# An encoder kernel whose body is built in an inner context that orders its instructions by another timing model

## The chip, the core and the metric

The kernel runs on one core of one Trainium2 chip. The metric is the device time of one execution in microseconds, as the median of several runs.

## The reference

A trunk of one layer is applied to two sequences, of 256 and 512 tokens, with 1024 channels. Cut to what matters:

```python
h = rmsnorm(x, norm_g)
q_a, k_a, v_a, z_a, qkv_b, z_b, a_b, b_b, gate = split(h @ w_in)
y_a = diff_branch(q_a, k_a, v_a, z_a, ...)      # 8 heads: rope, two softmaxes, w = p0 - lam * p1, w @ v
y_b = gdn_branch(qkv_b, z_b, a_b, b_b, ...)     # 8 heads: conv of width 4, gated delta rule, both directions
gates = sigmoid(gate)
merged = gates[0] * (y_a @ w_branch[0]) + gates[1] * (y_b @ w_branch[1])
y = rmsnorm(x + merged @ w_out, final_g)
```

The gated delta rule works in chunks: each chunk needs the inverse of a triangular matrix, and a state is carried from one chunk to the next, forwards and backwards.

## The kernel before

All 768 tokens are held together as the normed, transposed input `hT`, in two parts (high and low) whose products are added, so a projection costs three matmuls per block. A *unit* is one projection of 128 output channels: `load_split` (L152) loads a weight tile `raw` by a DMA on SP, ACT casts it to `whi` (L149), DVE subtracts to `wlo` (L150), and 24 pairs of matmuls (L197; `pa` of 256 columns, `pb` of 512) run into two accumulators; then an epilogue on ACT and DVE reads them. `raw`, `whi` and `wlo` have two buffers each, the accumulators four.

The projections are a background stream. `step_d` (L209) issues them under a priority counter of their own that starts at 1,000,000, so each ranks behind all other work; `fill` and `fill_to` place them in the text between the steps of the foreground, and `fill(1.3, True)` gives some of them the foreground's priority. The foreground is, in order: norm and transposes of the input; four pairs of heads of the gated delta rule (`gdn_pair`), each with a convolution (`conv`, L397: a scaled copy on ACT at L406, six taps on DVE at L410, a tanh at L413 and a product at L414), transposes of `kq` (L454), decays (`gb` fetched by DMA at L518, two POOL steps at L519 and L521, an exponential `ee` on ACT at L531), an inverse (`inverse`, L549) and a scan over chunks (`scan_round`, L684: `ps_s`, `ps_x`, `ps_o` on PE, `xd`, `xn`, `o` on ACT, `r`, `S`, `o` on DVE); then eight heads of attention; then the tail, where `load_y` (L968) loads the eight tiles of a branch's result (`yr`, two buffers) and splits them into `yh` and `yl`, the branch's projections run, and `out_proj` (L997) ends the kernel.

The text is not the order on the chip. A framework collects all instructions with their dependences and priorities and, when its context closes, walks through them with a model of the machine: whenever an engine is free in the model, the instruction of the lowest priority number whose inputs and buffers are ready in the model comes next on that engine, DMA issues included. What it yields is one fixed list of instructions for each engine, with semaphores; on the chip each engine takes its list in that order. The kernel before uses the framework's default model for this, which is the simpler one of two.

Of the kernel before, what the change touches and what calls it, by code (L numbers as in the profile page):

```python
# [41 lines left out]


@with_exitstack
def tile_trunk(
    ctx: ExitStack,
    tc: tile.TileContext,
    x_prompt, x_sample, norm_g, w_in, conv_w, lam_qk, diff_norm_g, a_log, dt_bias,
# [1033 lines left out]
    hes.close()  # L1082


# [1 line left out]
_INS = ["x_prompt", "x_sample", "norm_g", "w_in", "conv_w", "lam_qk", "diff_norm_g", "a_log", "dt_bias",  # L1086
        "gdn_norm_g", "w_branch", "w_out", "final_g"]
# [32 lines left out]
```

## Time and profile before

| | |
|---|---|
| median of 3 runs | 1219.04 us (1217.39 to 1221.33) |
| the profiled execution | 1223.08 us, span 1221.2 us, mean granted TensorE clock 0.992 |
| PE busy | 1178.3 us (96%), 7952 matmuls |
| PE weight loads busy | 1034.0 us (85%) |
| DVE busy | 746.4 us (61%) |
| ACT busy | 554.7 us (45%) |
| POOL busy | 122.7 us (10%) |
| DMA | 133.60 MB in 173063 packets, mean 109 GB/s |

The span is from the first to the last instruction that the profiler recorded; the execution's own time has 1.9 us around it. Matmuls are pipelined, so a busy PE is not PE at its peak. In the rows, L12 is line 12 of the kernel file, and out<-in names the tiles that an instruction writes and reads.

### The profile page before, as it was taken

How to read it: one execution, taken by the hardware profiler on the slowest of the kernel's cores; microseconds unless marked ns; L12 is line 12 of the kernel's file. 1: busy time of each engine (PE TensorE's matmuls, PEld its weight loads, DVE VectorE, ACT ScalarE, POOL GpSimd, SP SyncE). 2: the span in 40 equal slices, each digit the busy share in tenths (PEclk: the TensorE clock that was granted, in tenths of full speed). 3: DMA queues.
4: the chain of work that ended last, by engine and by line, in shares of the span. 5: the costliest groups of instructions: out<-in, count | busy, mean ns of one | idle time of the engine just before them, and what ended most of it. 6: DMA issues, size and time to landing. Idle time of an engine off the chain costs nothing. (4 is left out here: it accounts for less than half of the span.)

```text
span 1221.2 us, 20819 instructions
## 1 busy us (share of the span) xinstructions
PE 1178.3 (96%) x7952; PEld 1034.0 (85%) x7952; DVE 746.4 (61%) x1542; ACT 554.7 (45%) x1403; POOL 122.7 (10%) x210
## 2 busy tenths in 40 slices
PE   6979998999999998999999999999999999999997
PEld 5868888888888888888899889898898888878886
DVE  5568846675566846668254657767476645457332
ACT  6454445434662346722362546656465454332011
POOL 2222013200311022110000000000000000000000
PEclk9989999999999999999999999999999999999999
DMA  5213341345223451243425554353544548444231
GB/s 179 76 50 77 85 100 32 100 127 112 63 53 98 115 115 44 55 128 102 111 85 156 146 127 135 103 138 83 143 121 112 146 160 238 151 138 121 69 113 70
DMA packets 173063, 133.60 MB, mean 109 GB/s; under 512 B 53338, under 2 KB 147876, under 8 KB 172964
## 3 DMA queue, kind: packets, MB, share of 16 engines
q1 hardware_dynamic: 172832, 132.22, 38.7%
q8 instruction: 63, 1.03, 0.4%
q14 instruction: 36, 0.29, 0.1%
q10 hardware_dynamic: 132, 0.05, 0.0%
HBM read 89.72 MB, written 23.64 MB: 93 GB/s over the span
## 5 line engine op out<-in xcount | busy, mean ns | idle before, releaser
L197 PE MATMUL pb<-hT,whi 128*128 128x512 f32 x1152 | 432.7, 400 | 0.4 <-ACT hT L142 0.3
L197 PE MATMUL pa<-hT,whi 128*128 128x256 f32 x1152 | 322.6, 287 | 1.9 <-DVE gsp L240 1.9
L197 PEld LDWEIGHTS pb<-hT,whi 128*128 128x128 f32 x1152 | 216.6, 189 | 47.3 <-ACT hT L142 0.8
L197 PE MATMUL pb<-hT,wlo 128*128 128x512 f32 x576 | 230.3, 400 | 0.0
L197 PEld LDWEIGHTS pa<-hT,whi 128*128 128x128 f32 x1152 | 216.6, 190 | 5.3 <-DVE gsp L240 2.2
L149 ACT CAST whi<-raw 128x1024 fp32r<-128x1024 f32 x88 | 92.9, 1056 | 209.5 <-PE pb L197 204.0
L197 PE MATMUL pa<-hT,wlo 128*128 128x256 f32 x576 | 165.0, 287 | 0.1
L150 DVE TENSOR_TENSOR wlo<-raw,whi 128x1024 fp32r<-128x1024 f32 x88 | 108.3, 1230 | 71.9 <-ACT whi L149 67.1
L197 PEld LDWEIGHTS pb<-hT,wlo 128*128 128x128 f32 x576 | 108.7, 189 | 23.0
L197 PEld LDWEIGHTS pa<-hT,wlo 128*128 128x128 f32 x576 | 109.1, 189 | 1.6 <-DVE wlo L150 0.3
L410 DVE SCALAR_TENSOR_TENSOR kq<-xp,pcol,kq 128x258 f32<-128x258 f32 x96 | 55.7, 634 | 27.8 <-ACT kq L406 27.8
L197 PE MATMUL pv<-vhi,hT 128*128 128x256 f32 x384 | 72.2, 284 | 0.2 <-ACT xp L803 0.2
L897 ACT ACTIVATE pw<-ps_sc,st 128x512 f32<-128x512 f32 (+1 forms) x96 | 58.2, 619 | 30.8 <-DVE st L895 30.6
L299 POOL TENSOR_TENSOR oss<-oss,mhalf 128x6 f32<-128x6 f32 x16 | 22.6, 1415 | 439.5 <-DVE oss L298 439.5
L197 PEld LDWEIGHTS pv<-vhi,hT 128*128 128x128 f32 x384 | 60.1, 188 | 1.2 <-ACT xp L803 0.5
L895 DVE TENSOR_REDUCE st<-ps_sc 128x1 f32<-128x512 f32 (+1 forms) x80 | 51.5, 684 | 8.9 <-PE ps_sc L893 8.6
L197 PE MATMUL pv<-vlo,hT 128*128 128x256 f32 x192 | 54.4, 284 | 0.0
L584 DVE TENSOR_TENSOR inv<-inv 96x31 f32<-96x31 f32 (+15 forms) x124 | 41.9, 338 | 17.8 <-ACT inv L562 14.5
L197 PE MATMUL pb<-yh,whi 128*128 128x512 f32 x128 | 51.4, 402 | 0.0
L197 PE MATMUL pb<-yl,whi 128*128 128x512 f32 x128 | 51.0, 399 | 0.0
L197 PE MATMUL pb<-yh,wlo 128*128 128x512 f32 x128 | 50.7, 398 | 0.0
L1011 PE MATMUL po<-hT,mh 128*128 128x512 f32 (+1 forms) x156 | 45.4, 374 | 0.3 <-DVE gth L956 0.3
(288 smaller groups left out, 2202.8 us busy)
## 6 DMA issues: line engine op xcount, KB each, us to landing
raw<-in_w_in SPq DMA_DIRECT2D x72, 512.0 KB, 4.1
xx<-xp SPq DMA_DIRECT2D x64, 192.0 KB, 3.4
raw<-in_w_branch SPq DMA_DIRECT2D x16, 512.0 KB, 4.0
gb<-gcd SPq DMA_DIRECT2D x16, 384.0 KB, 3.6
gtd<-gsp SPq DMA_DIRECT2D x16, 384.0 KB, 2.7
th<-xp SPq DMA_DIRECT2D x64, 96.0 KB, 2.9
gth<-gtd SPq DMA_DIRECT2D x16, 384.0 KB, 4.1
vraw<-in_w_in SPq DMA_DIRECT2D x4, 1024.0 KB, 6.6
```

The costliest lines, as they stand in the source:

```text
L149: nc.scalar.copy(whi, raw)
L150: nc.vector.tensor_tensor(out=wlo, in0=raw, in1=whi.bitcast(F32), op=ALU.subtract)
L197: nc.tensor.matmul(out, l_, r_, start=st, stop=sp)
L299: nc.gpsimd.tensor_tensor(out=oss[:, 0, :], in0=oss[:, 1, :], in1=mhalf[:, :NCH], op=ALU.pow)
L410: nc.vector.scalar_tensor_tensor(out=dst[:, a:b], in0=xp[:, w + a:w + b], scalar=cw(w), in1=dst[:, a:b], op0=ALU.mult, op1=ALU.add)
L584: nc.vector.tensor_tensor(out=tmp[:, :n, :w], in0=L[:, j + 1:, j:j + 1].to_broadcast(shp), in1=X[:, j:j + 1, :w].to_broadcast(shp), op=ALU ...
L895: nc.vector.tensor_reduce(out=st[:, c, :G], in_=ps.rearrange("p (g s) -> p g s", g=G), axis=AX.X, op=ALU.max, negate=True)
L897: nc.scalar.activation(pw[:, c, S * g_:S * g_ + S], ps[:, S * g_:S * g_ + S], AF.Exp, bias=st[:, c, g_:g_ + 1], accum_out=sums[:, c, i:i + 1])
L1011: nc.tensor.matmul(ps[:, :c1 - c0], a[:, ts_], b[:, cs], start=f, stop=l)
```

## The change

The function that builds the body is renamed, and a new function of the old name opens a critical section in the given context and, inside it, a second context on the same core. The second context is told to order its instructions by the framework's timeline model (a model of the occupancy of engines, their queues and the DMA engines, and of TensorE's clock) and not by the default one. The body is built in the inner context, with the same text, tiles, buffers and priorities. For the outer context the critical section is one item that comprises all engines.

```diff
 @with_exitstack
-def tile_trunk(
+def trunk(
     ctx: ExitStack,
     tc: tile.TileContext,
     x_prompt, x_sample, norm_g, w_in, conv_w, lam_qk, diff_norm_g, a_log, dt_bias,
@@
     hes.close()
 
 
+def tile_trunk(tc, *args):
+    with tc.tile_critical(), tile.TileContext(tc.nc, schedule_with_timeline_sim=True) as inner:
+        trunk(inner, *args)
+
+
 # ---- launch: one core; inputs and outputs as the reference has them ----
```

## Rows read from the trace of the kernel before

**Rows 1.** The page: busy us of each engine, share of the span, instructions.

```profile
PE 1178.3 (96%) x7952; PEld 1034.0 (85%) x7952; DVE 746.4 (61%) x1542; ACT 554.7 (45%) x1403; POOL 122.7 (10%) x210
```

**Rows 2.** Windows of 40 us: window, length, busy (count) by engine, clock, DMA share, GB/s.

```profile
40.00:80.00 40.00, 32.53 (x180) 28.39 (x179) 23.46 (x49) 22.34 (x60) 13.21 (x20) 0.87 0.24 68
...
240.00:280.00 40.00, 40.00 (x233) 35.01 (x232) 26.29 (x68) 11.06 (x14) 1.78 (x4) 1.00 0.42 115
```

**Rows 3.** Timeline, start: start us, us, engine, line, what [idle before <-releaser].

```profile
0.81 0.20 POOL masks.py:197 MEMSET ident<- 128x128 f32 x1 [0.29 <-POOLq L1106]
...
7.26 0.45 PE L113 MATMUL ps_par<-ident,prow 128*128 128x128 f32 x1 [7.26 <-DMA prow<-in_diff_norm_g]
```

**Rows 4.** Timeline of the end.

```profile
1214.81 0.42 DVE L1012 TENSOR_TENSOR xres<-xres,po 128x256 f32<-128x256 f32 x1 [1.72 <-PE po L1011]
...
1216.90 1.41 DVE L1020 SCALAR_TENSOR_TENSOR sqf<-xres,ss,fg 128x512 f32<-128x512 f32 x2 [0.75 <-POOL ss L1017]
```

**Rows 5.** Waits of PE, 80 to 640: total us, times, longest; first and last of seven.

```profile
PE ps_x L715 <- ACT o L726: 2.6, 1, 2.6
...
PE ps_x L715 <- DVE v L546: 0.2, 1, 0.2
```

**Rows 6.** Waits of PE, 640 to 1000: first and last of five.

```profile
PE pa L197 <- DVE gsp L240: 1.9, 1, 1.9
...
PE pv L197 <- ACT xp L803: 0.2, 1, 0.2
```

**Rows 7.** Waits of PE, 1000 to 1222: first of three.

```profile
PE pa L197 <- ACT yh L975: 1.7, 1, 1.7
```

**Rows 8.** Timeline around the wait at 73.16.

```profile
61.49 0.32 SPq L518 DMA_DIRECT2D gb<-gcd  x1
...
62.45 0.59 ACT L402 COPY xp<-pb 128x512 f32<-128x512 f32 x1
...
65.17 1.48 POOL L519 TENSOR_TENSOR gb<-gb,NGC 128x768 f32<-128x768 f32 x1 [1.72 <-DMA gb<-gcd]
...
67.62 0.84 ACT L531 ACTIVATE ee<-gb 128x768 f32<-128x768 f32 x1 [2.89 <-POOL gb L521]
68.37 0.92 ACT L406 ACTIVATE kq<-xp,pcol 128x770 f32<-128x770 f32 x1
...
69.41 3.27 DVE L410 SCALAR_TENSOR_TENSOR kq<-xp,pcol,kq 128x258 f32<-128x258 f32 x6 [4.15 <-ACT kq L406]
...
73.16 0.66 PE L454 MATMUL ps_t<-ident,kq 128*128 128x128 f32 x2 [7.47 <-DVE kq L414]
```

**Rows 9.** Line L531: what ended ACT's idle time before it (us, times).

```profile
  POOL gb L521: 13.3, 6
```

**Rows 10.** Timeline of ACT in the first scan.

```profile
188.59 0.84 ACT L531 ACTIVATE ee<-gb 128x768 f32<-128x768 f32 x1 [2.21 <-POOL gb L521]
```

**Rows 11.** Windows around the wait at 73.16.

```profile
73.00:79.00 6.00, 5.84 (x23) 5.30 (x24) 3.43 (x9) 4.97 (x18) 0.00 (x0) 0.50 0.00 0
79.00:82.00 3.00, 3.00 (x18) 2.63 (x18) 2.88 (x6) 2.94 (x16) 0.17 (x3) 0.97 0.02 7
```

**Rows 12.** Line L154, the load of a weight tile: time to landing.

```profile
DMA to landing us min/median/max: 3.7/4.1/9.4
```

**Rows 13.** The page: costliest groups, busy us, mean ns | idle before.

```profile
L149 ACT CAST whi<-raw 128x1024 fp32r<-128x1024 f32 x88 | 92.9, 1056 | 209.5 <-PE pb L197 204.0
...
L150 DVE TENSOR_TENSOR wlo<-raw,whi 128x1024 fp32r<-128x1024 f32 x88 | 108.3, 1230 | 71.9 <-ACT whi L149 67.1
```

**Rows 14.** Tile `yr`: time to landing.

```profile
DMA to landing us min/median/max: 3.9/4.9/5.9
```

**Rows 15.** Groups of PE, 992 to 1016: count, busy us, mean ns | idle.

```profile
L197 PE MATMUL pb<-hT,whi 128*128 128x512 f32 x31 | 11.2, 394 | 0.0
...
L197 PE MATMUL pb<-hT,wlo 128*128 128x512 f32 x16 | 6.4, 399 | 0.0
```

**Rows 16.** Waits of SP's queue: total us, times, longest.

```profile
SPq L154 <- DVE gsp L240: 24.1, 1, 24.1
```

## The prediction

> **What bounds the kernel now.** Busy time by engine comes first [rows 1]: of a span of 1221.2 us PE is busy 1178.3, DVE 746.4, ACT 554.7. So PE is the limit on average and its idle time is 42.9 us in all. That is the size of what any order can move, because the change neither adds nor removes a matmul. Next, the windows of 40 us [rows 2] say where PE falls short: 7.5 us in 40 to 80, nothing in 240 to 280, where only projections and the setup of the recurrence run. Part of the rest is fixed: the first matmul starts at 7.26 us, after the DMA of its operand [rows 3], and the last ends about 1214.8, 6.4 us before the end of the span [rows 4], with the last norm and store behind it. Both are chains through single instructions, and no order shortens them much.
>
> The waits of PE by stage come next: 10.0 us from 80 to 640 (seven groups, [rows 5]), where the scan of the recurrence waits for ACT and DVE; 5.5 us from 640 to 1000 (five groups, [rows 6]); 2.3 us from 1000 on (three groups, [rows 7]). With the one wait of 7.47 us at 73.16 [rows 8] this makes 25.3 us in which PE waits for another engine in the middle of the kernel.
>
> **How one of these waits arises.** The largest is the one to understand, since it shows what the order does. ACT takes `ee` (L531) at 67.62, after 2.89 us in which it stands idle for POOL's `gb` [rows 8]. The copy of the convolution (L406) stands behind it on ACT, and its input was complete when L402 ended at 63.04. DVE then starts its six taps at 69.41, having waited 4.15 us for that copy, and PE's transposes of `kq` wait for DVE. An ordering that picks, at the moment when an engine is free, the ready instruction of lowest priority number would not leave ready work standing; so when it chose `ee` its own clock must have had `gb` done. In the trace `gb` was not: its DMA was issued at 61.49 and POOL could start at 65.17, 3.7 us later, and its two steps take until ACT's start at 67.62, 2.4 us more. Over the kernel ACT stands idle before `ee` for 13.3 us, six times [rows 9], and a second of them, at 188.59, delays what stands behind it on ACT [rows 10], L726 among it, and with that the 2.6 us wait that heads [rows 5]. These are errors of the planner's durations, and durations are what the change replaces.
>
> **The change part by part.** Instructions, tiles, buffers, priorities and data stay. Three things differ.
>
> *The order.* It is chosen again on every engine and on the SP queue. I cost it by the waits it can remove.
> (a) The wait at 73.16. It costs 7.47 us, and a slower clock after it: the granted clock is 0.50 (1.2 GHz) from 73 to 79, after those 7.5 us without a matmul, and 0.97 again from 79 to 82 [rows 11]. Work of 6 us at half speed would take 3 us at 2.4 GHz, so 3.0 us more. Bounds 0 and 10.5; I take all of it, because the misjudged durations (a DMA of 3.7 us, two POOL instructions) are plain ones that a fuller model should have nearer.
> (b) The 10.0 us in the scans. Bounds 0 and 10.0; I take half, 5.0. Some are of this kind (the 2.6 us), others are links of the recurrence (`xd`, `xn`, `ma`) for which PE had no projection ready, and a better clock brings no work.
> (c) The 5.5 us of attention. Bounds 0 and 5.5; I take 2.0. The largest, 1.9 us, is a projection waiting for an accumulator that DVE has not read.
> (d) The 2.3 us of the tail, bounds 0 and 2.3; I take nothing, as they wait for loads that come one behind the other.
> (e) The new order's own waits. A model differs from the chip too, and every choice is made without looking ahead. Nothing in the trace prices this; below it is 0, above it is the 25.3 us that the present planner's errors cost. I take 4, near the lower end, since about 10.5 of those 25.3 stem from one kind of error.
>
> *The nesting.* The critical section encloses the whole body, so there is one more meeting of the engines at either end. Below, the one that the trace shows at the start: POOL is held 0.29 us [rows 3]. Above, all that follows the last DVE instruction, 1221.2 - 1218.3 = 2.9 us for the final store and the close [rows 4]. I take 1.5 us, in between; nothing hides it, as PE has no work there.
>
> *The DMA order.* Nearly all transfers are issued from SP in one order, so a transfer that waits holds those behind it. A weight tile lands in 4.1 us (median, [rows 12]) and takes 1.06 us on ACT and 1.23 us on DVE [rows 13], 6.4 us; a unit of 24 pairs of matmuls takes PE 24 x 0.343 = 8.2 us (40 us hold 233 matmuls, 116.5 pairs, [rows 2]). With two buffers of each stage the load can be up to two units ahead, so 16.4 - 6.4 = 10 us of delay is covered. I cost it at nothing, and as a rival if that cover goes.
>
> **Sum.** Against its own time, 1223.08 us (1221.2 of span and 1.9 around it): - 10.5 - 5.0 - 2.0 + 4.0 + 1.5 = - 12.0, so 1211.1 us under the profile's conditions. That execution is 4.0 us above the median of the runs, 1219.04, so I state the result as 1219.0 - 12.0 = 1207 us.
>
> **A rule set against the rows.** In 240 to 280, where PE never idles, weight loads are busy 35.01 of 40 us, 87.5% [rows 2]; over the whole kernel 1034.0 of 1221.2, 84.7% [rows 1]. If all of it ran as densely as that stretch it would take 1034.0 / 0.875 = 1181.5 us, so 39.7 us is the ceiling of any order, start and end included. The Trainium skill (Perfetto Trace Analysis, Identifying the Most-Contended Engine) says that matmul busy time is a poor measure of distance to the limit and that weight-load busy time is a good one. Read literally that leaves 15% of the span to be won (rival 4 below); the row of the dense stretch says that 12.5 of these 15.3 points are not to be had, and the trace decides.
>
> **The rivals.**
> 1. *Errors are exchanged, not removed.* The new order avoids the wait at 73.16 but makes others of the same size: (e) at 14 to 18 instead of 4. Speaking for it: 25.3 us of waits in 1221 is already little, 2.1%, and every model errs. Time: 1207 + 12 = 1219. Chance 0.13. That the order hardly differs (priorities and dependences fix it) belongs here too, with the nesting alone: 1220.5, chance 0.04. Against it: ACT's place for `ee` can only come from modelled durations.
> 2. *Slower by a cover used up.* At 992 the attention is over and the eight loads of `ybd` run in a chain: 4.9 us each with two buffers [rows 14], so some 20 us for eight. PE does not notice, because 47 pairs of projection matmuls are left (31 and 16, [rows 15]), 47 x 0.343 = 16.1 us. If the new order spends them earlier, in the waits of (b) and (c) and beyond them, PE stands up to 16.1 us and then runs at half clock for some 3 us worth, as after 73: 1207 + 19 = 1226. It passes 1222.7 when more than 13.2 of the 16.1 us are gone. For it: these matmuls have the highest numbers, that is the lowest priority, and an ordering that believes in longer waits uses them up sooner. Against it: what is spent earlier must have filled something, and only 15.5 us of waits lie between 80 and 1000. Chance 0.14.
> 3. *Slower by the SP queue.* A transfer that waits is placed ahead of a weight load for longer than the 10 us of cover. One such case stands in the trace: L154 behind `gsp`, 24.1 us [rows 16]; a wait of that length where PE has no slack costs 24.1 - 10 = 14 us. It decides from the first: 1221 with one, 1235 with two. For it: the queue is shared by nearly everything. Against it: a model with better transfer times should see just this. Chance 0.15, at 1235.
> 4. *All the time in which no weights load is to be had*, 1221.2 - 1034.0 = 187 us [rows 1], and the time nears 1034: the dense stretch above speaks against it; chance 0.01.
>
> **How the numbers follow.** The forecast, 1207 us, has 0.53; its own range is 1194 to 1215. A measurement of this kernel can tell about 0.3%, 3.7 us, from no change: faster is below 1215.4, slower above 1222.7. Faster: 0.53 + 0.01 = 0.54 and nothing of the others. Same: 0.17 from rival 1, as its times lie around 1219. Slower: 0.14 + 0.15 = 0.29. The low end is all of (a) to (d) won, 28.3 us, with 0.3 for the nesting: 1219 - 28 = 1191. The high end takes in rivals 2 and 3 with two waits and the nesting at its upper bound: 1235 + 1.4, and a few us for a third lesser wait, 1240.
>
> **What would show it.** (a) holds if PE has no wait of several us between 60 and 80 and the clock stays at 1.00 there; it fails if ACT still stands before `ee` for some 3 us. (b): fewer than 5 us of waits in the scans, with projection matmuls between `ps_x` and `ps_o`. (e): new names among PE's waits, under 5 us in sum. Nesting: more than 0.29 us before the first DMA and more than 3 us behind the last DVE instruction. Rival 2 shows as a gap of PE before `pa<-yh` with few `hT` pairs after the last `ps_yt`; rival 3 as PE waiting for `whi` or `wlo` while the load behind them was issued late. The prediction would be wrong above all if the new order makes PE wait for reasons that the present one does not have.

## The result, and the profile after

The changed kernel takes 1343.26 us (median of 4, 1342.33 to 1344.04), the kernel before, run beside it, 1220.14. The ratio is 1.1012, 95% interval 1.099 to 1.1035: 10% slower, where 1207 us was forecast and 1240 was the end of the range. The profiled execution took 1343.6 us with a span of 1341.1.

Busy time of the changed kernel, from the page; the answer to [rows 1]:

```profile
PE 1211.7 (90%) x7952; PEld 1062.5 (79%) x7952; DVE 741.0 (55%) x1542; ACT 557.7 (42%) x1403; POOL 114.3 (9%) x210
```

The instructions are the same ones (7952 matmuls), and DVE and ACT are as busy as before. PE stands idle for 1341.1 - 1211.7 = 129.4 us instead of 42.9, 86.5 more, and it is busy 33.4 us longer with the same matmuls, because more of them run at the slow clock. Four windows say where. They are, for the kernel before, start and first setup, recurrence, attention, tail (columns: window and its length, busy us and instructions of PE, PEld, DVE, ACT and POOL, granted clock of TensorE, DMA share, GB/s):

```profile
0.00:89.60 89.60, 71.60 (x382) 59.42 (x383) 53.28 (x114) 50.52 (x122) 21.83 (x51) 0.94 0.34 103
89.60:633.60 544.00, 533.34 (x4052) 467.43 (x4051) 360.06 (x892) 252.66 (x688) 82.92 (x143) 1.00 0.35 90
633.60:985.50 351.90, 348.16 (x2318) 314.30 (x2317) 221.54 (x383) 184.94 (x483) 13.33 (x9) 1.00 0.46 126
985.50:1221.20 235.70, 225.20 (x1207) 192.86 (x1206) 111.55 (x155) 66.61 (x110) 4.58 (x7) 0.99 0.41 132
```

and the same four stages of the changed kernel:

```profile
0.00:88.00 88.00, 76.00 (x435) 64.47 (x435) 54.20 (x115) 52.14 (x125) 19.57 (x50) 1.00 0.38 111
88.00:734.20 646.20, 569.58 (x4123) 499.72 (x4122) 355.97 (x899) 259.33 (x698) 77.81 (x145) 0.92 0.31 79
734.20:1114.10 379.90, 355.82 (x2312) 322.61 (x2312) 230.11 (x388) 191.23 (x491) 12.33 (x9) 0.96 0.45 122
1114.10:1341.10 227.00, 210.32 (x1089) 175.67 (x1087) 100.68 (x141) 54.97 (x90) 4.59 (x7) 0.96 0.37 117
```

The first stage is better: 53 matmuls more in 1.6 us less, at full clock. Most of the loss is in the recurrence: 102 us longer (with 71 matmuls more in it), PE idle 76.6 us instead of 10.7, clock 0.92 instead of 1.00. Attention has 24.1 us of idle instead of 3.7, the tail 16.7 instead of 10.5. The waits of PE in the changed kernel (groups as in [rows 5 to 7]: us in total, times, longest):

```profile
PE ps_y L668 <- ACT P L659: 17.0, 3, 8.2
PE ps_t L454 <- ACT kn L458: 15.1, 6, 4.3
PE ps_p L618 <- DMA XY<-sX: 13.0, 2, 12.8
PE ps_par L113 <- DMA prow<-in_diff_norm_g: 10.1, 1, 10.1
PE ps_pv L926 <- ACT wT L917: 9.0, 4, 4.1
PE ps_yt L307 <- DVE o L300: 6.0, 1, 6.0
```

Apart from `ps_par` at the start, these are names that hardly occur in the kernel before, and all of them are foreground steps: the wait of a projection would read `pa`, `pb` or `pv`. (Such waits come next in the list: 5.7 us for `gsp`, 5.3 for `vhi`, 5.0 for `zt`.) So look at the projections, PE's background work. The windows below count the matmuls of L197 alone, in the first pair's scan and in the second pair's setup; kernel before, then changed kernel (PE and PEld busy, count, clock, DMA):

```profile
179.10:210.80 31.70, 6.03 (x18) 3.06 (x18) 0.95 0.14 43
210.80:233.60 22.80, 13.94 (x65) 9.95 (x65) 1.00 0.31 99
```

```profile
202.10:264.10 62.00, 45.21 (x233) 35.43 (x232) 1.00 0.24 69
264.10:286.60 22.50, 0.60 (x2) 0.31 (x3) 0.77 0.18 59
```

The scan of the first pair now holds 233 projection matmuls instead of 18 and takes 62.0 us instead of 31.7. The setup behind it has 2 left instead of 65. Nothing is lost inside this scan: PE is busy for all of the 62.0 us, and at its end 1006 projection matmuls are done at 264.3 us where the kernel before had done 690 at 210.9. The 316 more are worth 54.2 us at 0.343 us a pair, and they took 53.4 us, so the two kernels are level there. The loss comes behind it. The setup looks like this over all engines, before and after:

```profile
210.80:233.60 22.80, 22.70 (x138) 19.01 (x136) 15.33 (x44) 15.34 (x75) 5.32 (x5) 1.00 0.31 99
```

```profile
264.10:286.60 22.50, 15.24 (x76) 11.85 (x76) 13.99 (x42) 14.67 (x73) 6.01 (x4) 0.77 0.18 59
```

The two take as long, but in the first PE was full and got 65 projection matmuls done on the side; in the second it stands 7.3 us, and the clock falls. The same happens at the next two pairs (6.1 us of idle each, clock 0.76 and 0.80). An estimate by the same 0.343 us for each pair done ahead puts the changed kernel 23 us behind the kernel before at the end of the second scan, 45 at the end of the third and 80 at the end of the fourth.

Projections are not used up for good in these setups, since hundreds of them run later; those next in line cannot start. Two finished ones hold the four accumulators until their tile `zt` is free, and `zt` is freed by the store of the pair before, which stands behind the late output transposes:

```profile
281.56 1.55 SPq L310 DMA_DIRECT2D ybd<-zt  x2
...
285.64 0.41 DVE L240 SCALAR_TENSOR_TENSOR zt<-th,pa 128x256 f32<-128x256 f32 x1
...
286.62 0.59 PE L197 MATMUL pa<-hT,whi 128*128 128x256 f32 x2
```

PE starts no projection from 265 until this one at 286.62, and the setup is all but over by then.

How the projections get into the scan shows in the timeline of the changed kernel:

```profile
208.62 0.62 ACT L734 ACTIVATE xd<-ps_x,sc__889 128x128 f32<-128x128 f32 x2 [0.76 <-PE ps_x L715]
209.13 0.37 ACT L737 COPY xn<-ps_x 128x256 f32<-128x256 f32 x1
209.23 0.48 PE L197 MATMUL pb<-hT,whi 128*128 128x512 f32 x1
...
212.01 0.28 PE L197 MATMUL pa<-hT,wlo 128*128 128x256 f32 x1
212.13 0.61 PE L744 MATMUL ps_o<-xd,kn 128*128 128x128 f32 x4
```

`xd` and `xn` are complete at 209.50. The matmuls of `ps_o` that read them start at 212.13, behind 2.6 us of projections. The order was fixed before the run, so in the model's own clock the two copies must have been done later than they are on the chip. (That is an inference; no run here changed what the model takes for ACT or PE.)

### The profile page after: what moved, and what is told of

Same layout as the page of the kernel before. It is cut to its first block, busy times and chain, and to the rows that moved or that the text cites. A ratio compares the mean times of both kernels' runs of the same rounds, so it can differ in the third digit from the quotient of the medians.

```text
span 1341.1 us, 20877 instructions
## 1 busy us (share of the span) xinstructions
PE 1211.7 (90%) x7952; PEld 1062.5 (79%) x7952; DVE 741.0 (55%) x1542; ACT 557.7 (42%) x1403; POOL 114.3 (9%) x210
## 5 line engine op out<-in xcount | busy, mean ns | idle before, releaser
L197 PE MATMUL pb<-hT,whi 128*128 128x512 f32 x1152 | 430.9, 402 | 0.0
L197 PE MATMUL pa<-hT,whi 128*128 128x256 f32 x1152 | 315.7, 287 | 10.8 <-DVE gsp L240 5.7
L197 PEld LDWEIGHTS pb<-hT,whi 128*128 128x128 f32 x1152 | 217.8, 190 | 46.7 <-DVE gsp L241 0.3
L197 PE MATMUL pb<-hT,wlo 128*128 128x512 f32 x576 | 231.1, 401 | 0.0
L197 PEld LDWEIGHTS pa<-hT,whi 128*128 128x128 f32 x1152 | 217.8, 193 | 15.0 <-DVE gsp L240 5.9
L197 PE MATMUL pa<-hT,wlo 128*128 128x256 f32 x576 | 165.6, 287 | 0.4 <-DVE wlo L150 0.4
L150 DVE TENSOR_TENSOR wlo<-raw,whi 128x1024 fp32r<-128x1024 f32 x88 | 107.4, 1222 | 89.8 <-ACT whi L149 88.7
L197 PEld LDWEIGHTS pb<-hT,wlo 128*128 128x128 f32 x576 | 109.4, 190 | 24.4
L197 PEld LDWEIGHTS pa<-hT,wlo 128*128 128x128 f32 x576 | 110.8, 192 | 2.6 <-DVE wlo L150 1.0
L197 PE MATMUL pv<-vhi,hT 128*128 128x256 f32 x384 | 74.9, 291 | 5.3 <-ACT vhi L149 5.3
L197 PEld LDWEIGHTS pv<-vhi,hT 128*128 128x128 f32 x384 | 62.3, 196 | 6.2 <-ACT vhi L149 5.5
L410 DVE SCALAR_TENSOR_TENSOR kq<-xp,pcol,kq 128x258 f32<-128x258 f32 (+1 forms) x96 | 53.9, 612 | 2.6 <-ACT kq L406 2.6
L197 PE MATMUL pv<-vlo,hT 128*128 128x256 f32 x192 | 55.1, 288 | 0.0
L197 PE MATMUL pb<-yl,whi 128*128 128x512 f32 x128 | 51.3, 401 | 0.0
L197 PE MATMUL pb<-yh,wlo 128*128 128x512 f32 x128 | 51.3, 401 | 0.0
L197 PE MATMUL pb<-yh,whi 128*128 128x512 f32 x128 | 51.2, 405 | 0.0
L817 ACT CAST hl<-xx 128x1536 fp32r<-128x1536 f32 x16 | 23.6, 1476 | 58.0 <-DMA xx<-xp 58.0
```

The costliest lines, as they stand in the source:

```text
L150: nc.vector.tensor_tensor(out=wlo, in0=raw, in1=whi.bitcast(F32), op=ALU.subtract)
L197: nc.tensor.matmul(out, l_, r_, start=st, stop=sp)
L410: nc.vector.scalar_tensor_tensor(out=dst[:, a:b], in0=xp[:, w + a:w + b], scalar=cw(w), in1=dst[:, a:b], op0=ALU.mult, op1=ALU.add)
L817: nc.scalar.copy(hl, xx)
```

## The experiments

Two theories stood against each other. **A, cover:** the order spends the projections inside the scans, where the chain hardly needs them, and the stages behind them wait. **B, foreground:** the order places ACT and DVE work wrongly, whatever the projections do. A third suspect was the nesting.

**e1, the nesting alone; e2, the model alone.**

```diff
-    with tc.tile_critical(), tile.TileContext(tc.nc, schedule_with_timeline_sim=True) as inner:
+    with tc.tile_critical(), tile.TileContext(tc.nc) as inner:              # e1
-    with tile.TileContext(nc) as tc:
+    with tile.TileContext(nc, schedule_with_timeline_sim=True) as tc:       # e2, on the kernel before
```

> The critical section and the inner context stay, but the inner context uses the default model; the list of every engine is then the one of the kernel before. Theory A (the new order alone makes the 123 us): 1220 to 1225 us. Theory B (in the nested context each transfer takes longer to issue on SP, 0.63 us instead of 0.38 for a weight tile, and the order is innocent): about 1340. Theory C (order and issue both cost): 1230 to 1300.

> No nesting: the one context is told to use the timeline model. The lists are those of the changed kernel. Theory A: about 1340 us, with issues on SP as short as before. Theory B: 1207 to 1220. Theory C: 1230 to 1300, and the sum of this excess and that of the nesting alone gives about 123 us or less.

e1: 1229.07 us, ratio 1.0076 (1.0056 to 1.0097). e2: 1308.9 us, ratio 1.0737 (1.0716 to 1.0759). Each lies a little outside what theory C gave, but both parts cost, as C has it. The kernel before took 1219.61 beside them, so the order alone costs 89.3 us and the nesting alone 9.5. Together they cost 123.1, which is 24.3 more than the sum. The instruction order of e1 is that of before on every engine and that of e2 is that of the changed kernel, so the 9.5 us are no matter of order.

**e3 and e4, what the nesting changes.** In the program built, 440 of the 568 transfers carry a mark for a short issue. In the inner context none does. A switch of the framework takes the mark away without nesting:

```diff
+    nc.dge_precook = False      # e3 on the kernel before, e4 on e2
```

> The kernel before, without nesting, with its order, but with every transfer kept off the short issue path (a switch of the framework); nothing else differs. If what the nesting costs is the issue time of transfers: the same time as the nesting alone, within 3 us. If the nesting costs by its own meetings of engines: 1220, and the nesting alone is above it.

> No nesting, timeline model, and every transfer kept off the short issue path, so that the planner plans with the issue times that the transfers then have; its lists differ from those of the changed kernel. If the changed kernel is slow because its order was made for short issues that it does not get: well below 1343, 1250 or less. If long issues cost under any order: 1320 to 1345.

e3: 1230.54 us, ratio 1.008 (1.0055 to 1.0104), the time of e1. e4: 1300.66, ratio 1.0664 (1.0646 to 1.0683), between what its two theories gave (1250 or less, 1320 to 1345). One line of the trace shows the difference, the 64 transfers of `ma<-sY` on SP (issue in ns: shortest, median, longest); before, changed kernel, e1, e3:

```profile
L612 SPq DMA_DIRECT2D ma<-sY x64: 385/439/2119, 155.6 to 596.7; - x64
```

```profile
L612 SPq DMA_DIRECT2D ma<-sY x64: 557/604/1617, 170.7 to 703.8; - x64
```

```profile
L612 SPq DMA_DIRECT2D ma<-sY x64: 555/604/1597, 157.3 to 602.8; - x64
```

```profile
L612 SPq DMA_DIRECT2D ma<-sY x64: 555/604/1778, 158.5 to 607.4; - x64
```

So the price of the nesting is the longer issue, as far as the times can tell: e1 and e3 differ by 1.5 us, which is within the noise. What the prediction had priced as two meetings of the engines can be seen in the trace all the same. In e1 the first DMA is issued at 1.04 us instead of 0.81, and from the end of the last DVE instruction to the end of the span it takes 5.0 us (1224.6 less 1219.57), against 3.2 in e3 (1229.0 less 1225.80) and 2.9 before [rows 4]; e1, then e3:

```profile
1218.15 1.42 DVE L1020 SCALAR_TENSOR_TENSOR sqf<-xres,ss,fg 128x512 f32<-128x512 f32 x2 [0.75 <-POOL ss L1017]
```

```profile
1224.38 1.42 DVE L1020 SCALAR_TENSOR_TENSOR sqf<-xres,ss,fg 128x512 f32<-128x512 f32 x2 [0.75 <-POOL ss L1017]
```

e4 was ordered with the long issues known to the planner and is 42.6 us faster than the changed kernel, which has the same long issues but the order of e2. That fits the 24.3 us: the changed kernel runs an order that was chosen for issues it does not get. It does not measure them, since the order of e4 was planned anew and differs in other places too. What grows from e2 to the changed kernel, with the same order, is above all the wait that heads the list, from 9.0 to 17.0 us. The two rows of e2:

```profile
PE ps_p L618 <- DMA XY<-sX: 9.3, 1, 9.3
PE ps_y L668 <- ACT P L659: 9.0, 3, 4.0
```

In the first inverse the sixteen transfers `ma<-sY` take SP 11.63 us instead of 9.48, the loads of `gb` stand behind them, and ACT stands idle before `ee` for 11.39 us instead of 6.92, with the copies `P` behind it. The longest single wait, 12.8 us at 690, owes less to the long issues, as e2 has 9.3 of it:

```profile
682.45 1.26 SPq L601 DMA_DIRECT2D XY<-sX  x2
...
685.10 2.41 SPq L602 DMA_DIRECT2D XY<-sY  x3
687.58 1.26 SPq L601 DMA_DIRECT2D XY<-sX  x2
688.88 0.62 SPq L602 DMA_DIRECT2D XY<-sY  x1
689.55 2.61 SPq L606 DMA_DIRECT2D X<-sX  x4
690.21 3.08 PE L618 MATMUL ps_p<-XY,MA 64*64 64x32 f32 x48 [12.81 <-DMA XY<-sX]
```

SP needs 0.6 us for each of a dozen transfers on which PE waits, and no projection is left to cover them.

**e5, the model's order with the projections held out of the scans.**

```diff
+    HELD = {n: 0 for n in range(16, 21)} | {n: 1 for n in range(28, 33)} | {n: 2 for n in range(40, 45)}
...
+        if n in HELD:
+            nc.scalar.activation(whi, raw, AF.Copy, scale=gate[HELD[n]])
+        else:
+            nc.scalar.copy(whi, raw)
...
         scan(hd, gp, more)
+        if p < 3:
+            gate[p] = const.tile([P, 1], F32, name=f"gate{p}")
+            nc.vector.tensor_scalar(gate[p], hd[1]["o"][:, 5, 0:1], 0.0, 1.0, op0=ALU.mult, op1=ALU.add)
```

> The model's order alone (no nesting), in which some projections cannot start inside a scan: their weights' split (L149) is scaled by a constant 1.0 that is written when the scan of the pair before has ended. The order built this way has 15, 0, 0 and 26 projection matmuls in the four scans, where the order without it has 232, 66, 90 and 0, and 129, 129 and 131 in the setups of pairs 1 to 3, where that has 2, 0 and 27. Theory A (the model spends the projections, which are PE's cover, inside the scans, where the chain hardly needs them, and the stages behind wait): the three setups wait 2 to 4 us instead of 11 to 12, the waits of the later stages shrink too, 30 to 70 us come back of the 89, so 1235 to 1275 us. Rival B (the model misorders ACT and DVE work ahead of what PE needs, wherever the projections are): the setups still wait, 1295 us or more.

1277.73 us, ratio 1.0472 (1.044 to 1.0504): 31.2 us of the 89.3 come back, of the 30 to 70 that A gave, and the time lies just past the slow end of its range (1275). The first scan and the setup behind it, all engines:

```profile
191.40:222.50 31.10, 27.29 (x210) 24.91 (x209) 21.72 (x65) 18.14 (x65) 3.42 (x10) 1.00 0.04 14
222.50:256.80 34.30, 33.17 (x204) 29.12 (x201) 20.81 (x54) 18.87 (x77) 7.37 (x8) 1.00 0.40 111
```

The setup is full again (33.17 of 34.30 us, clock 1.00), as A says, and its waits are gone. The scan is nearly that of the kernel before: 31.1 us with 17 projection matmuls and 3.8 us of idle, where that had 31.7, 18 and 3.5. What is left stands elsewhere: in the waits of this kernel `ps_y <- ACT P` comes first with 12.8 us. A is right and not the whole.

**e6, the output transposes earlier.**

```diff
         c1, c2, c3, c8 = gp
+        flush()
...
-        flush()
         for g_, H in enumerate(hd):
             H["ma"] = ma = ...
```

> The model's order alone, with the call that empties the list of late output transposes (it frees the z tiles, for which two finished projections wait) at the start of each pair instead of behind its setup. The order built has 93, 88 and 82 projection matmuls in the setups of pairs 1 to 3 instead of 2, 0 and 27; the scans are as full of projections as before (232, 19, 24). Theory A (cover): the setups' waits of 11 to 12 us fall to 2 to 4, but the projections are then missing elsewhere: 10 to 30 us faster than the model's order, 1279 to 1299. Rival B (misordered ACT and DVE work): no gain over 5 us, 1304 to 1314.

1297.74 us, ratio 1.0633 (1.0609 to 1.0657), 11.2 us better than e2: the low end of A. The projections come back into the setups once `zt` is free earlier, but two waits show why the gain is small, the first of them made by the edit, which now asks for `o` at once:

```profile
PE ps_yt L307 <- DVE o L300: 22.2, 7, 5.9
PE ps_p L618 <- DMA XY<-sX: 15.4, 2, 14.1
```

**e7, the other way round: the kernel before, with only its scans made to yield to projections.**

```diff
-                        nc.tensor.matmul(ps[...], H["kq"][...], H["S"][seq, d], start=True, stop=True)
+                        yielding(lambda: nc.tensor.matmul(ps[...], ...))     # issued with priority 2000000 and on
```

> The order of before, with one thing of the model's order put in: in the scans the ps_s matmuls (L698) get a priority number behind the projections. The order built has 336, 144, 144 and 0 projection matmuls in the four scans (before: 18, 16, 16, 20) and 0 in each of the setups of pairs 1 to 3 (before: 65, 174, 174). No timeline model. Theory A (cover spent in the scans): most of what the model's order loses appears here too, 1270 to 1310 us, with waits of 8 to 12 us in each of the three setups. Rival B (the model's ACT and DVE orders cost the time): within 15 us of before, 1215 to 1235.

1300.44 us, ratio 1.066 (1.0626 to 1.0694). With the simple planner and everything else as before, 80 us are lost, and the two stages look like those of the changed kernel (all engines; the first window begins 2.5 us ahead of the scan):

```profile
175.90:269.00 93.10, 86.69 (x549) 77.85 (x545) 35.15 (x80) 33.60 (x86) 8.77 (x12) 0.96 0.28 81
269.00:291.30 22.30, 15.20 (x74) 12.25 (x72) 12.97 (x41) 13.90 (x72) 5.29 (x4) 0.77 0.09 36
```

15.20 us busy at clock 0.77 in the setup, with no projection in it, against 15.24 at 0.77 in the changed kernel. Here too `zt` holds the projections back: behind each of the three setups the next one waits 5.4 us for it. Spending the cover in the scans is enough to lose this much; B is not needed for it. The edit holds the scans up more (91 us for the first), so 80 us is no measure of A's share in e2.

**e8 and e11, the first 90 us in the kernel before.** e8 tests step (a) by itself, e11 puts the model's placement of the first transposes into the old order.

```diff
+            pr = tc.cur_priority
+            if p == 0:
+                tc.cur_priority = state["prio"]
             nc.scalar.activation(ee[:, g_, d], gb, AF.Exp)                   # e8
+            tc.cur_priority = pr
...
+                        pr = tc.cur_priority
+                        if not p:
+                            tc.cur_priority = state["prio"]
                         nc.tensor.transpose(ps[:, 128 * q:...], kqt[...], ident)   # e11, L454
+                        tc.cur_priority = pr
```

> The order of before, with the priority of the first pair's exponentials ee (L531) moved behind the convolution's work, so that on ACT the copy L406 stands ahead of the second pair of them. A test of step (a) of the prediction by itself: if the wait of 7.47 us at 73.16 us comes from that order on ACT, and the clock of 0.50 behind it from the wait, 5 to 11 us go, 1209 to 1215 us. If the setup is bound by DVE's taps instead, the wait only moves: 1217 to 1221 us.

> The order of before, with the transposes ps_t of the first pair (L454) behind the projections queued until then in priority: 194 projection matmuls stand ahead of the first of them, as in the model's order, where before has 86; every later stage keeps its projections within 18. In the model's order this stage and the one before it waited 12.7 us together, in before 23.1. If that comes from this placement, 5 to 10 us are gained: 1209 to 1215 us, faster than both kernels. If the setup then ends later and the first inverse with it, no change: 1217 to 1222.

e8: 1220.01 us, ratio 0.9993 (0.9978 to 1.0008), no change, as its second theory had it. ACT's copy now stands ahead of the second pair of exponentials, and the wait for `kq` only shrinks from 7.5 to 5.4 us:

```profile
PE ps_t L454 <- DVE kq L414: 5.4, 1, 5.4
```

e11: 1217.3 us, ratio 0.997 (0.9951 to 0.9988), some 0.3% faster than before and the only kernel here that beats both. That is 2.0 us, less than the 5 to 10 of its first theory and within the range of its second.

**e9, ACT's order of `ee` and `P`.** In e5, ACT in the inverse of the first pair (here L541 is L531, L669 is L659, L681 is L671):

```profile
175.75 0.48 ACT L669 COPY P<-ps_p 128x384 f32<-128x384 f32 x1
182.43 0.84 ACT L541 ACTIVATE ee<-gb 128x768 f32<-128x768 f32 x1 [6.20 <-POOL gb L531]
183.18 0.46 ACT L669 COPY P<-ps_p 128x384 f32<-128x384 f32 x1
```

ACT stands for 6.2 us at `ee` while the second copy `P`, which PE needs, waits behind it. The Trainium skill (TensorE: Matmul & The Clock Gate, "Architectural detail: the array is 16× 32×32, not 1× 128×128") says that ACT and DVE work through their queues strictly in order; these three lines agree for ACT.

```diff
-            nc.scalar.activation(ee[:, g_, d], gb, AF.Exp)
+            nc.scalar.activation(ee[:, g_, d], gb, AF.Exp, scale=gate["e", p] if p else 1.0)
```

where `gate["e", p]` is a constant 1.0, written behind the inverse from `ma`.

> The kernel of e5_model_hold, in which ee of pairs 1 to 3 (L531) cannot start on ACT before the inverse of the pair before has ended: its scale is a constant 1.0 written then. On ACT both copies P (L659) now stand ahead of ee in every pair, as in before; in e5 an ee stands between or ahead of them in all three. Theory A' (a second cost of the model's order: it takes gb as ready too early, ACT stands at ee, and the copy P that PE needs stands behind it): the wait of ps_y for P, 12.8 us in three places in e5, falls to under 2, and 8 to 13 us go: 1264 to 1270 us. Rival: the scan behind needs ACT just as much and the wait only moves: 1273 to 1281.

1264.33 us, ratio 1.0372 (1.0351 to 1.0394), 13.4 us better than e5, as Theory A' had it. Both copies now run together, and no wait for `P` is left:

```profile
176.70 0.86 ACT L672 COPY P<-ps_p 128x384 f32<-128x384 f32 x2
```

**e10 and e12, the cover of the later stages.** Both hold further projections: e10 one to the end of the last scan and three to the middle of the last head, e12 two to the end of the last head.

```diff
+    | {50: 3, 73: 4, 74: 5, 75: 5}     # e10, added to HELD of e9; attention_head(h, ap, 3.0)
+    | {74: 3, 75: 3}                   # e12, the same; attention_head(h, ap, 2.0)
```

> The kernel of e9_hold_ee, in which also one projection is held to the end of the last scan and three to the middle of the last head, by the same kind of scale, and the projections are queued later in the program (3.0 instead of 4.7 for each tile of a head). The order built has 48 projection matmuls more between the last scan and the first head, and 10 more behind the last head. Theory A (cover): the 9 to 10 us of waits between the last scan and the first head fall to 2 to 5, 4 to 10 us faster than e9. Rival (that wait is for the first head's own operands, which come no earlier): no difference to e9 over 3 us.

> The kernel of e9_hold_ee, in which the last two projections cannot start before the last head has its last sums (the same kind of scale; for that the projections are queued later in the program, 2.0 instead of 4.7 for each tile of a head). The order built has 48 projection matmuls, 8 us of PE's work, behind the last matmul of the heads, where e9 has none and before has 118. Theory A (the model's order has used up this cover too; the prediction's rival 2): the wait of 6.9 us for o behind the last head goes or falls under 2, and 5 to 9 us come back, 1255 to 1260 us. If the heads then lack what is held for the end, the waits move into the last head: 1262 to 1267.

e10: 1263.15 us, ratio 1.0357 (1.0336 to 1.0379), no difference to e9: PE idles 2.6 us instead of 5.3 between the last scan and the first head, but the wait for `o` behind the last head grows from 6.9 to 8.6. e12: 1268.47 us, ratio 1.0394 (1.0352 to 1.0435), 4 us worse, a miss: the wait of 6.9 us behind the last head is gone, but from the first head to the last PE idles 19.5 us instead of 11.1, and in the tail it waits 6.2 us for `yh` instead of 1.7. Here is what e9 is left with, in the four stages:

```profile
0.00:86.90 86.90, 76.81 (x434) 64.93 (x435) 54.72 (x116) 52.35 (x125) 20.43 (x50) 1.00 0.37 112
86.90:670.50 583.60, 554.11 (x4124) 486.53 (x4122) 365.42 (x904) 261.18 (x698) 82.49 (x145) 0.99 0.34 87
670.50:1037.00 366.50, 350.13 (x2312) 319.06 (x2311) 228.21 (x387) 190.59 (x490) 12.27 (x9) 0.97 0.46 126
1037.00:1261.50 224.50, 208.47 (x1089) 175.55 (x1087) 101.42 (x142) 55.36 (x91) 4.58 (x7) 0.96 0.37 119
```

The 45.0 us to the kernel before (1264.33 - 1219.28) are spread: 29.5 us of idle in the recurrence against 10.7, 16.4 in attention against 3.7, 16.0 behind it against 10.5, and slower clocks. One piece has a name: in the first scan ACT still stands 3.65 us before an `ee` at 193.55, and PE then waits 4.8 us for `xd`. The cause of the rest stays open. The model's order of ACT and DVE in the scans and the heads is the obvious suspect, and it was not tried by itself.

Each of e4 to e6, e9, e10 and e12 was planned anew, so its order differs from its neighbour's in more than the edit. e4, where only the issues changed, came out 8 us faster than e2. A difference of that size is worth only as much as the wait that goes with it in the trace: e5 and e9 have theirs (the waits of the setups, the wait for `P`); the 31.2 and 13.4 us are what the edits brought in all.

## Why the prediction was wrong

**The price, in sum.** The order costs 89.3 us, the nesting with its longer DMA issues 9.5, and both together 24.3 more, most likely because the order was chosen for short issues and runs with long ones. Of the 89.3, 31.2 came back when the projections were held out of the scans and 13.4 when `ee` no longer stood ahead of `P`; 45 stay open.

**(a), the wait at 73: it went, but not for the reason given.** PE is never idle from 40 to 80 in the changed kernel, at full clock, where [rows 2] had 32.53 us of 40:

```profile
40.00:80.00 40.00, 40.00 (x242) 33.97 (x240) 28.65 (x68) 26.94 (x75) 7.91 (x18) 1.00 0.30 81
```

By the end of the first setup 282 projection matmuls are done at 88.0 us instead of 231 at 89.6. That is 25.5 pairs of 0.343 us and 1.6 us, 10.3 us, where 10.5 was forecast, so within this stage the size came out. The reason did not. A fuller model was to have the durations before `ee` nearer; in its order ACT stands idle before `ee` for more than three times as long as in [rows 9] (changed kernel; in e2, with short issues, it is 32.1 us in nine waits):

```profile
  POOL gb L521: 43.9, 9
```

What took the wait at 73 away is that the model's order starts this setup 19 us later, with 194 projection matmuls ahead of it instead of 86. e11 did that alone in the old order and won 2.0 us of the whole time, and e8, which moved `ee` on ACT, won nothing. In the changed kernel the lead of 10.3 us is gone by the end of the first scan, behind a wait of 8.2 us for `P` among others. So no run shows that the 10.5 us of this stage were there to be had at the end of the kernel, and that the stage's sum fits is in part luck.

**(b) and (c), the waits of the scans and heads: wrong in sign.** The prediction asked for projection matmuls between `ps_x` and `ps_o` as the mark of success. They came, 233 in the first scan, and were the damage: PE's idle time there had been 3.5 us, so for the most part they did not fill waits but stood in front of foreground matmuls whose operands were ready.

**(e), the new order's own waits: the step that failed.** It was taken at 4 us with a bound of 25.3, "the 25.3 us that the present planner's errors cost". For the order, (a) to (e) sum to 13.5 us gained; e2 measured 89.3 lost. That bound is no bound, and neither are the 42.9 us of idle time that the prediction took as the size of what any order can move: they limit what an order can win, and the changed kernel added 86.5. The 25.3 is what errors cost while the cover is intact, and the same chains without projections beside them cost far more: a setup hides its whole chain when 65 projection matmuls stand by, and shows 7.3 us of idle and a clock of 0.77 when they have been spent. What had to be priced was the foreground chain of each stage without its cover, three setups, four inverses and the heads.

**Rival 2 was the right mechanism in the wrong place.** It said that an order that believes in longer waits uses the projections up sooner, and looked for it at the load of `ybd` only, at 19 us. Its argument against itself, "what is spent earlier must have filled something, and only 15.5 us of waits lie between 80 and 1000", is the error in one sentence: projections can also be spent by delaying work that is ready, as e7 shows with the old planner. At the place it named it came true too: 118 projection matmuls lay behind the last head before, none in the changed kernel, and PE waits there for `o`, 6.0 us.

**The nesting: 1.5 us forecast, with bounds of 0.3 and 2.9; 9.5 measured.** The two meetings are in the trace of e1 at about the size forecast (0.2 us at the start, some 2 at the end), too small to show between the times of e1 and e3. Another path for issuing DMAs, which no row of before could show and the sum left out, cost the rest. That the parts do not simply add, by 24.3 us here, was not priced either.

**The DMA order at nothing, and rival 3.** For the projections' `whi` and `wlo` the cover of 10 us held; the one larger wait for weights is 5.3 us for `vhi`, once. SP did become late, but by the longer issues of the inverse's own transfers (11.63 us instead of 9.48 for sixteen of them, with `gb` behind), not by a load behind a waiting transfer.

## What to carry to other kernels

Low-priority work that fills an engine's waits is a stock, and an order can spend it where it buys nothing. Before pricing a new order, count that work in each stage (what can start there, given the buffers, and not what is left in all), and price every stage's chain without it; the waits visible today are no upper bound. When a wrapper is put around a kernel, run the wrapper alone first: here it changed how transfers are issued, and the order had been chosen for the other way.

## What was not expected of the hardware

The same transfer takes SP 0.439 us or 0.604 us (median of 64 each, L612) depending on how its issue was prepared, while the median time from issue to landing moves only from 2.0 to 2.2 us. The Trainium skill (Perfetto Trace Analysis, "DMA Instruction — HWDGE (DVE, Sync)") says that the time shown on the issuing queue covers the making of descriptors and not the movement of data, and these two medians agree. Some 9.5 us in 1220 hung on it, though SP is no engine that the page counts as busy.

And matmul busy time rose by 33.4 us, 1178.3 to 1211.7, for the same 7952 matmuls: each of the three setups that ran dry pulled the granted clock down (0.77, 0.76 and 0.80 as means of the levels 1.2 and 2.4 GHz), and the work behind the gaps ran slower.
